# One state tile per direction in the RWKV-7 mixer, and its decays' running sums as TensorE products

## The chip, the cores and the metric

One core of a Trainium2 chip runs the whole kernel in one launch. The metric is device microseconds of that core, the median of three runs. TensorE is PE in the profile's rows, VectorE is DVE, ScalarE ACT, GpSimd POOL, SyncE SP; SP issues the loads.

## The reference, cut to what matters

A backbone of two layers over 256 context and 256 latent tokens, 1024 wide. Layer 0 is a Mamba-2 mixer with a dense SwiGLU, layer 1 a bidirectional RWKV-7 mixer ("mixer 2") with a top-2-of-8 expert SwiGLU. The change touches mixer 2 alone. For each direction d and each of 16 heads of 64 it computes

```python
logw = -0.606531 * sigmoid(w0[d] + tanh(xw @ w1[d]) @ w2[d])
a    = sigmoid(a0[d] + (xa @ a1[d]) @ a2[d])
kd   = k * (1 + (a - 1) * k_a)
...
sa = einsum('bhvk,bhk->bhv', S, kk_t)
S  = S * w_t - sa * (kk_t * a_t) + v_t * kd_t       # w_t = exp(logw_t)
y  = einsum('bhvk,bhk->bhv', S, r_t)
```

once over the context tokens, of which only the final states are kept, and once over the latent tokens, which start from these.

## The kernel before, in words

Mixer 2 works on 256 tokens in four chunks of 64 (c = 0 to 3 forwards, 3 to 0 backwards), on eight heads at a time (half hh, four tiles of 128 features, two heads of 64 in each: "par" 0 in rows 0 to 63 and par 1 in rows 64 to 127, `ROWS`). A unit j, hh is the context (j = 0) or the latent tokens (j = 1) with one half of the heads. Each unit has three parts. **A** (`stage`) makes the decays and the operands of all chunks and their gram matrices. **T** (`invert`) inverts the 64x64 triangular systems, a long chain of small VectorE steps and TensorE products. **S** (`scan`) takes the state through the four chunks. Several of these generators are woven by `weave`, and a scheduler then orders each engine's queue. The stages of the program are named by what is woven, with j and hh behind each letter: A00 (with the v features), A01T00, T01S00, F1S01 (with the features of the latent tokens), A10, T10, S10A11, T11, S11, then `finish` and the experts. S11 is woven with the output projection, which `finish` ends.

Part A, lines 1005 to 1113 of before. `lora(pi)` makes, for a pair of chunks (128 tokens), th = tanh of the w path and ta = tanh of the a path, with features on the partitions: for each of four feature tiles a product with hw (line 1013) and one with ha (line 1014), each followed by its own ScalarE tanh with the bias w0h (lines 1015, 1017). GpSimd makes th + 1 (line 1023). `decays(c)` then forms the running sum of th over the 64 tokens of one chunk with a VectorE scan (line 1043; smask restarts it at each tile), and ScalarE makes from it the decays Dp (line 1047), dc (line 1049) and the inverse (line 1050). `operands` multiplies these into KR and BK, `grams` (lines 1082, 1091) makes C and BT.

Part S, lines 1227 to 1288. The state of one direction is held in two tiles, Sz[d][0] with the heads of par 0 in rows 0 to 63 and zeros below, and Sz[d][1] the other way round; xz is held in the same way. Thus every product takes all 128 rows as its contraction and writes the 64 output rows of its head's half. For a step and direction: x = C^T Q + KR^T Sz into PSUM, copied to xz by VectorE (par 0, line 1245) and ScalarE (par 1, line 1246); u = Tt^T xz, copied to Q (lines 1263, 1264); the next state is a TensorE copy of Sz by an identity (two products of 256 columns) plus BT^T Q, scaled by dc into Sz (line 1274, twice). On latent tokens, also an output y.

The lora weights w_l2 come by SP (line 1305), in A00 into half of the tile "Tt"; the head selector hT (line 1365) goes into the other half and is read by `unit_keys` (line 841), which normalises the keys. `decay` and `rate` (lines 902, 919) write the factors hw and ha, 64 rows for each direction in 128-row tiles whose other rows are zero.

Of the kernel before, what the change touches and what calls it, by code (L numbers as in the profile page):

```python
# [19 lines left out]
D = 1024  # L20
# [45 lines left out]
def prepare(inp):  # L66
# [46 lines left out]
    a["w_l2"] = np.stack([g["rw_w2"][0].reshape(128, D), g["rw_a2"][0].reshape(128, D), g["rw_g2"][0]], axis=1)  # L113
# [24 lines left out]
def tile_backbone(ctx: ExitStack, tc: tile.TileContext, T, out: bass.AP, dbg=None, stop=99):  # L138
# [584 lines left out]
    for t in Sz[0] + Sz[1] + xz[0] + xz[1]:  # L723
        G.memset(t, 0.0)
# [121 lines left out]
    def features(up, F, names, MB, nraw, nsp, base, normed_all=None, vx=None, xs=None, later_x=None, raw=None, part=None, tail=None, eng=(V, G)):  # L846
# [55 lines left out]
        def decay(o):  # L902
            for d in range(2):
                S.activation(F["hw"][d][ROWS[d]], o[ROWS[d], :256], AF.Tanh)
# [12 lines left out]
            return late  # L917

        def rate(o):
            for d in range(2):  # L920
                S.copy(F["ha"][d][ROWS[d]], o[ROWS[d], :256])
# [74 lines left out]
    def stage(tp, rp, F, un, d, l2, nb, bks, tags, ready):  # L996
# [8 lines left out]
        def lora(pi):  # L1005
            ts = slice(128 * pi, 128 * pi + 128)
            th = tp.tile([128, 2, 4, 64], F32, name=f"th{d}")
            ta = tp.tile([128, 4, 128], F32, name=f"ta{d}", bufs=nb)
            kd = tp.tile([128, 4, 128], F32, name=f"kd{d}", bufs=nb)
            for i in range(4):  # L1010
# [11 lines left out]
                yield  # L1022
# [16 lines left out]
        def decays(c):  # L1039
            th = cur[c // 2][0]  # L1040
            cum = tp.tile([128, 4, 64], F32, name=f"cum{d}", bufs=2)
            e = 1 if d == 0 else -1
            V.tensor_tensor_scan(cum.rearrange("p k t -> p (k t)")[:, ::e], smask.rearrange("p k t -> p (k t)"),
                                 th[:, c % 2].rearrange("p k t -> p (k t)")[:, ::e], 0.0, op0=ALU.mult, op1=ALU.add)
            Dp = tp.tile([128, 4, 65], F32, name=f"Dp{d}", bufs=2)
            G.memset(Dp[:, :, 64 * d:64 * d + 1], 1.0)
            S.activation(Dp[:, :, o:o + 64], cum, AF.Exp, scale=-0.3032655)
            end = 63 * o
            S.activation(un.dc[d][:, :, c:c + 1], cum[:, :, end:end + 1], AF.Exp, scale=-0.3032655)
            S.activation(cum, cum, AF.Exp, scale=0.3032655)  # L1050
            return Dp, cum

        def operands(c, dd, slot):
            Dp, Di = dd
# [12 lines left out]
            return BK  # L1067
# [33 lines left out]
        dd = decays(od[0])  # L1101
        yield
        for i, c in enumerate(od):
            while not ready(i):
                yield
            BK = operands(c, dd, 2 * i + d)
            if i % 2 == 0 and j:
                bonus(od[i] // 2)
            if i == 1:
                yield from lora(od[2] // 2)  # L1110
            if i < 3:
                dd = decays(od[i + 1])
            yield
            yield from grams(c, BK, 2 * i + d)
# [112 lines left out]
    def scan(F, un, y=None):  # L1227
# [6 lines left out]
        for i in range(4):  # L1234
            st = []
            for d in range(2):
# [13 lines left out]
            for d in range(2):  # L1250
# [4 lines left out]
                if not (j and i == 3):  # L1255
                    for par in range(2):
                        mm(ba[ROWS[par], 0:256], ident[:, ROWS[par]], Z[par][:, ks, :].rearrange("p h v -> p (h v)"), first=True)
                if j:
                    for h, par in HP:
                        mm(py[ROWS[par], h, :], Z[par][:, k0 + h, :], KR[:, h, 64:128], first=i == 3 and h == 0)  # L1260
                for h, par in HP:
                    mm(pu[ROWS[par], h, :], un.Tt[:, d, 4 * c + h, :], xz[d][par][:, h, :], end=h == 3)
# [39 lines left out]
    def stages(tp, rp, F, un, nb, bks, tags, ready, l2=None):  # L1302
        if l2 is None:
            l2 = tp.tile([128, 2, 512], F32, name="l2")
        SY.dma_start(l2, T["w_l2"][:, :2, 512 * un.hh:512 * un.hh + 512])
# [12 lines left out]
    with ExitStack() as es:  # L1318
        f0 = es.enter_context(tc.tile_pool(name="f0", bufs=1, reuse_waits="tile"))
        F = {n: f0.tile([128, 8, 256], F32, name=n) for n in ("k", "kk")}  # L1320
        F.update({n: [f0.tile([128, 256], F32, name=f"{n}{d}") for d in range(2)] for n in ("hw", "ha")})
        for t in F["hw"] + F["ha"]:
            G.memset(t, 0.0)
# [23 lines left out]
        with tc.tile_pool(name="r00", bufs=1, side="right", reuse_waits="tile") as r00, tc.tile_pool(name="tp0", bufs=1, reuse_waits="tile") as tp:  # L1347
# [15 lines left out]
            l2 = held[:, 1].rearrange("p (a b) t -> p a (b t)", a=2)  # L1363
            hT = held[:16, 0].rearrange("p (k a) t -> p k (a t)", k=8)
# [7 lines left out]
            slots = {"T": ("BK00", [128, 1024]), "M0": ("l2", [128, 2, 512]), "M1": ("BK01", [128, 1024])}  # L1372
# [8 lines left out]
    if True:  # L1381
# [3 lines left out]
        F.update({n: [fk.tile([128, 256], F32, name=f"{n}{d}") for d in range(2)] for n in ("hw", "ha")})  # L1385
        for t in F["hw"] + F["ha"]:
            G.memset(t, 0.0)
# [12 lines left out]
        for d in range(2):  # L1400
            dump(f"S{d}", Sz[d][0])
# [130 lines left out]
    def start_half():  # L1532
# [3 lines left out]
        later(g2, T["w_l2"][:, 2, :], after)  # L1536
# [326 lines left out]
```

## Time and profile before

| | us |
|---|---|
| median of three runs | 2649.88 |
| lowest and highest | 2646.11, 2653.32 |
| the profiled execution's own time | 2658.37 |
| its span in the trace | 2656.5 |
| TensorE busy | 2440.9 (92%) |
| VectorE busy | 2039.1 (77%) |
| ScalarE busy | 1457.5 (55%) |
| GpSimd busy | 341.9 (13%) |

The stages of mixer 2 stand in the trace at about these times: A00 985 to 1048, A01T00 to 1128, T01S00 to 1180, F1S01 to 1300, A10 to 1345, T10 to 1410, S10A11 to 1470, T11 to 1540, S11 to 1592 us. Layer 0 stands before 930 us, the experts after 1640. The granted clock of TensorE has two levels, 1.2 and 2.4 GHz; the profile gives it as a share of the higher one, so a stage's mean of 0.62 is a stretch mostly at the lower level. Read a timeline by its starts: the duration given for a group of matmuls contains a modelled tail of 0.2 to 0.3 us, and the next group may start within it.

### The profile page before, as it was taken

What the parts mean: (1) busy time and instruction counts of PE and PEld (TensorE: products, weight loads), DVE (VectorE), ACT (ScalarE), POOL (GpSimd) and SP (SyncE); (2) the same over time, 40 slices, a digit from 0 to 9 for tenths busy, and PEclk for the clock granted to TensorE, in tenths of its full rate; (3) what the DMA queues carried; (4) which work ended last, traced back from release to release, by engine and by line L of the source; (5) the groups of instructions that cost most, each with busy time, mean ns of one, the idle gap of its engine ahead of it and who ended that gap; (6) DMA issues with size and microseconds to landing.
All of it is one profiled execution on the core that took longest, in us unless ns stands there. A gap on an engine that the chain in (4) does not pass through costs nothing. (4 is left out here: it accounts for less than half of the span.)

```text
span 2656.5 us, 44879 instructions
## 1 busy us (share of the span) xinstructions
PE 2440.9 (92%) x17770; PEld 1994.8 (75%) x17770; DVE 2039.1 (77%) x3070; ACT 1457.5 (55%) x2322; POOL 341.9 (13%) x434
## 2 busy tenths in 40 slices
PE   7999998999999978679868797999999999999997
PEld 4777776878888767568767686887888788878875
DVE  5787888667554377687676645999999899989997
ACT  4454545333223265435335225877787777778775
POOL 1011102000000254233432211000000000000001
PEclk9999999999999978577888687999999999999999
DMA  7323232336564221022020116899999899989994
GB/s 260 120 88 102 74 104 80 122 121 201 169 203 140 85 94 48 16 68 80 18 73 2 59 39 265 318 359 341 359 370 358 327 363 368 357 320 368 367 340 158
DMA packets 99211, 511.63 MB, mean 193 GB/s; under 512 B 11648, under 2 KB 19072, under 8 KB 55216
## 3 DMA queue, kind: packets, MB, share of 16 engines
q1 hardware_dynamic: 97520, 506.52, 52.8%
q8 instruction: 141, 2.31, 0.4%
q10 hardware_dynamic: 1472, 2.16, 0.3%
q14 instruction: 78, 0.64, 0.1%
HBM read 506.54 MB, written 2.10 MB: 191 GB/s over the span
## 5 line engine op out<-in xcount | busy, mean ns | idle before, releaser
L1720 DVE TENSOR_TENSOR wlo<-wraw,whi 128x1024 fp32r<-128x1024 f32 x662 | 798.4, 1224 | 69.6 <-ACT whi L1719 49.1
L1719 ACT CAST whi<-wraw 128x1024 fp32r<-128x1024 f32 x662 | 694.3, 1051 | 207.1 <-PE gu L214 111.9
L213 PE MATMUL gu<-wlo,xg 128*128 128x512 f32 x896 | 355.3, 397 | 1.5 <-DVE wlo L1720 0.7
L214 PE MATMUL gu<-whi,xg 128*128 128x512 f32 x896 | 349.8, 391 | 0.0
L212 PE MATMUL gu<-whi,xg 128*128 128x512 f32 x896 | 336.4, 392 | 1.1 <-ACT xg L1739 0.9
L206 ACT CAST whi<-wraw 128x1024 fp32r<-128x1024 f32 (+2 forms) x126 | 129.7, 1030 | 218.4 <-PE acc L213 206.2
L207 DVE TENSOR_TENSOR wlo<-wraw,whi 128x1024 fp32r<-128x1024 f32 (+2 forms) x126 | 151.8, 1205 | 110.0 <-ACT whi L206 109.8
L213 PEld LDWEIGHTS gu<-wlo,xg 128*128 128x128 f32 x896 | 168.5, 188 | 42.3 <-DVE wlo L1720 6.1
L212 PEld LDWEIGHTS gu<-whi,xg 128*128 128x128 f32 x896 | 168.4, 188 | 38.1 <-ACT xg L1739 1.6
L214 PEld LDWEIGHTS gu<-whi,xg 128*128 128x128 f32 x896 | 168.7, 188 | 31.5
L213 PE MATMUL y<-wlo,HT 128*128 128x512 f32 x448 | 178.4, 398 | 2.3 <-DVE wlo L1720 2.0
L212 PE MATMUL y<-whi,HT 128*128 128x512 f32 x448 | 176.6, 396 | 3.0 <-DVE xg L1740 3.0
L214 PE MATMUL y<-whi,HT 128*128 128x512 f32 x448 | 176.1, 393 | 0.0
L212 PE MATMUL acc<-h2hi,whi 128*128 128x512 f32 x352 | 137.4, 393 | 3.4 <-ACT h2hi L343 3.4
L1794 POOL TENSOR_TENSOR wraw<-yx,SH 128x512 f32<-128x512 f32 x4 | 7.5, 1875 | 1022.1 <-DVE yx L1790 1022.1
L213 PE MATMUL acc<-h2lo,whi 128*128 128x512 f32 x352 | 137.4, 391 | 0.0
L212 PE MATMUL acc<-hhi,whi 128*128 128x512 f32 (+1 forms) x328 | 135.8, 414 | 0.8 <-ACT whi L206 0.8
L214 PE MATMUL acc<-h2hi,wlo 128*128 128x512 f32 x352 | 134.7, 391 | 0.3 <-DVE wlo L207 0.3
L213 PE MATMUL acc<-hlo,whi 128*128 128x512 f32 (+1 forms) x328 | 134.1, 409 | 0.0
L214 PE MATMUL acc<-hhi,wlo 128*128 128x512 f32 (+1 forms) x328 | 133.6, 408 | 0.0
L305 POOL TENSOR_TENSOR sqa<-sqa,sq 128x512 f32<-128x512 f32 (+1 forms) x35 | 47.5, 1357 | 579.2 <-issue 311.3
L260 DVE SCALAR_TENSOR_TENSOR wraw<-wraw,scb 128x1024 f32<-128x1024 f32 x56 | 68.5, 1223 | 50.2 <-DMA wraw<-in_w_modT_dram 49.4
(565 smaller groups left out, 5358.5 us busy)
## 6 DMA issues: line engine op xcount, KB each, us to landing
wraw<-in_w_mi_dram SPq DMA_DIRECT2D x219, 1024.0 KB, 5.0
wraw<-in_w_mo_dram SPq DMA_DIRECT2D x112, 1024.0 KB, 5.0
wraw<-in_w_modT_dram SPq DMA_DIRECT2D x56, 512.0 KB, 3.9
wraw<-in_w_ffi_dram SPq DMA_DIRECT2D x44, 512.0 KB, 3.6
wraw<-in_w_mod_dram SPq DMA_DIRECT2D x40, 512.0 KB, 5.0
wraw<-in_w_mb_dram SPq DMA_DIRECT2D x40, 512.0 KB, 4.8
wraw<-in_w_mbo_dram SPq DMA_DIRECT2D x16, 512.0 KB, 4.1
wraw<-in_w_ffo_dram SPq DMA_DIRECT2D x16, 512.0 KB, 3.6
```

Of the source, the lines that this page charges most:

```text
L206: S.copy(hi, raw)
L207: eng[q % len(eng)].tensor_sub(lo, raw, hi.bitcast(F32))
L212: PE.matmul(o, whi, xhi, start=start, stop=False)
L213: PE.matmul(o, whi, xlo, start=False, stop=False)
L214: PE.matmul(o, wlo, xhi, start=False, stop=stop)
L260: V.scalar_tensor_tensor(t, w, 0.5, scb[:, j, :], op0=ALU.mult, op1=ALU.mult, accum_out=mods[l][:, n, j:j + 1])
L305: G.tensor_add(self.acc, self.acc, sq)
L1719: S.copy(hi, raw[:, k:k + 2, :])
L1720: V.tensor_sub(lo, raw[:, k:k + 2, :], hi.bitcast(F32))
L1794: G.tensor_mul(xf[:, tt, 512 * n:512 * n + 512], fs, fg[:, 512 * n:512 * n + 512])
```

## The change

In part A: w0 and a0 become a 65th row of w_l2, against a row of ones in hw and ha, so that the tanh needs no bias. hw of both directions and ha lie in rows 0 to 63. One product of 128x512 (line 1012 of after) gives the w path with tokens on the partitions, four of 128x128 give the a path in one bank, and each has one tanh of 128x512. The running sums are four products for a pair of chunks and a direction, of th with a constant triangular matrix (tb_f, tb_b, line 1049); the three exponents read their PSUM bank, 512 wide, once for two chunks. The scan's mask and the w0h constants go. In part S: one Sz and one xz tile for each direction, the two halves below each other; products with them contract over the 64 rows of their head; xz is copied by heads (VectorE two, ScalarE two, 128 rows each); one copy product and one update of 128x256 for a step and direction. The head selector goes into the tile "M1".

```diff
+    a["w_l2"] = np.stack([np.stack([np.concatenate([g["rw_" + n + "2"][0][d], g["rw_" + n + "0"][0][d][None]])
+                                    for n in ("w", "a")], axis=1) for d in range(2)], axis=1)
...
+    same = (j < 64) == first
+    for n, v in (("tb_f", same & (r <= cc)), ("tb_b", same & (r >= cc)), ("m_f0", mf * sign[0]), ("m_f1", mf * sign[1]), ("m_b0", mb * sign[0]), ("m_b1", mb * sign[1]),
...
-    Sz = [[rc.tile([128, 8, 64], F32, name=f"Sz{d}{par}") for par in range(2)] for d in range(2)]
-    xz = [[rc.tile([128, 4, 64], F32, name=f"xz{d}{par}") for par in range(2)] for d in range(2)]
+    Sz = [rc.tile([128, 8, 64], F32, name=f"Sz{d}") for d in range(2)]
+    xz = [rc.tile([128, 4, 64], F32, name=f"xz{d}") for d in range(2)]
...
+            p = ms()
+            PE.matmul(p, F["hw"][d][:, ts], l2[:65, d, 0], start=True, stop=True)
+            S.activation(flat(th), p, AF.Tanh, scale=0.5)
+            p = ms()
+            for i in range(4):
+                PE.matmul(p[:, 128 * i:128 * i + 128], l2[:65, d, 1, 128 * i:128 * i + 128], F["ha"][d][:, ts],
+                          start=True, stop=True)
+            S.activation(flat(ta), p, AF.Tanh, scale=0.5)
+            yield
             for i in range(4):
                 k = k0 + i
-                p = ms()
-                PE.matmul(p[:, 0:128], l2[:, 0, 128 * i:128 * i + 128], F["hw"][d][:, ts], start=True, stop=True)
-                PE.matmul(p[:, 128:256], l2[:, 1, 128 * i:128 * i + 128], F["ha"][d][:, ts], start=True, stop=True)
-                S.activation(th[:, :, i, :], p[:, 0:128].rearrange("p (c t) -> p c t", c=2), AF.Tanh,
-                             bias=w0h[:, 8 * d + k:8 * d + k + 1], scale=0.5)
-                S.activation(ta[:, i, :], p[:, 128:256], AF.Tanh, bias=w0h[:, 16 + 8 * d + k:17 + 8 * d + k], scale=0.5)
...
-            V.tensor_tensor_scan(cum.rearrange("p k t -> p (k t)")[:, ::e], smask.rearrange("p k t -> p (k t)"),
-                                 th[:, c % 2].rearrange("p k t -> p (k t)")[:, ::e], 0.0, op0=ALU.mult, op1=ALU.add)
...
+        def decays(pi):
+
+            th = cur[pi][0]
+            p = ms()
+            for i in range(4):
+                PE.matmul(p[:, 128 * i:128 * i + 128], th[:, i, :], K2["tb_" + "fb"[d]], start=True, stop=True)
+            cum = p.rearrange("p (k c t) -> p k c t", k=4, c=2)
...
+            S.activation(Dp[:, :, :, o:o + 64], cum, AF.Exp, scale=-0.3032655)
+            S.activation(un.dc[d][:, :, 2 * pi:2 * pi + 2], cum[:, :, :, 63 * o], AF.Exp, scale=-0.3032655)
...
+            S.activation(Di, cum, AF.Exp, scale=0.3032655)
...
-                    mm(px[ROWS[par], h, :], KR[:, h, 0:64], Z[par][:, k0 + h, :], end=h == 3)
-                V.tensor_copy(xz[d][0][ROWS[0]], px[ROWS[0]])
-                S.copy(xz[d][1][ROWS[1]], px[ROWS[1]])
+                    mm(px[ROWS[par], h, :], KR[ROWS[par], h, 0:64], Z[ROWS[par], k0 + h, :], end=h == 3)
+                V.tensor_copy(xz[d][:, 0:2], px[:, 0:2])
+                S.copy(xz[d][:, 2:4], px[:, 2:4])
...
-                    for par in range(2):
-                        mm(ba[ROWS[par], 0:256], ident[:, ROWS[par]], Z[par][:, ks, :].rearrange("p h v -> p (h v)"), first=True)
+                    mm(ba[:, 0:256], ident, Z[:, ks, :].rearrange("p h v -> p (h v)"), first=True)
...
-                    mm(pu[ROWS[par], h, :], un.Tt[:, d, 4 * c + h, :], xz[d][par][:, h, :], end=h == 3)
+                    mm(pu[ROWS[par], h, :], un.Tt[ROWS[par], d, 4 * c + h, :], xz[d][ROWS[par], h, :], end=h == 3)
...
-                    for par in range(2):
-                        V.tensor_tensor(Z[par][ROWS[par], ks], pz[ROWS[par]],
-                                        un.dc[d][ROWS[par], :, c:c + 1].to_broadcast([64, 4, 64]), op=ALU.mult)
+                    V.tensor_tensor(Z[:, ks], pz, un.dc[d][:, :, c:c + 1].to_broadcast([128, 4, 64]), op=ALU.mult)
...
-            hT = held[:16, 0].rearrange("p (k a) t -> p k (a t)", k=8)
+            hT = tp.tile([128, 1024], F32, name="M1")[:16].rearrange("p (k f) -> p k f", k=8)
```

The scheduler orders each queue anew. The first place is TensorE near the end of S11, where the state products (xu from Sz and KR, line 1233 before and 1238 after) of the last step meet the output products (acc from C and Q). Before, all of them contract over 128 rows:

```order
L1233 MATMUL xu<-Sz_7482,KR_14504 64x64
L1233 MATMUL acc<-C_12284,Q_12270 64x64
L1233 MATMUL xu<-Sz_7481,KR_14504 64x64
L1233 MATMUL acc<-C_12285,Q_12271 64x64
L1233 MATMUL xu<-Sz_7482,KR_14504 64x64
L1233 MATMUL acc<-C_12284,Q_12270 64x64
L1233 MATMUL xu<-Sz_7481,KR_14504 64x64
L1233 MATMUL acc<-C_12285,Q_12271 64x64
```

After, at the same place, the products with Sz contract over 64 rows and those with C still over 128:

```order
L1238 MATMUL xu<-Sz_7476,KR_14222 64x64
L1238 MATMUL acc<-C_12126,Q_12112 64x64
L1238 MATMUL xu<-Sz_7476,KR_14222 64x64
L1238 MATMUL acc<-C_12127,Q_12113 64x64
L1238 MATMUL xu<-Sz_7476,KR_14222 64x64
L1238 MATMUL acc<-C_12126,Q_12112 64x64
L1238 MATMUL xu<-Sz_7476,KR_14222 64x64
L1238 MATMUL acc<-C_12127,Q_12113 64x64
```

The two kinds take turns in both orders; what moved is the shape, which now changes at every row. Counted over the whole program, the shape of consecutive products (contraction and output rows, in steps of 32, 64 and 128) changes 459 times before and 616 times after.

The second place is TensorE in A01T00, where the inversion's products (line 1192 before, 1197 after: ms from M and T) share the queue with the lora products of the second pair of chunks (1013, 1014; after 1012, 1016) and, after, with the running sums (1049: xu from the constants c and th). Before:

```order
L1192 MATMUL ms<-M_9414,T 32x16 x18
L1013 MATMUL xu<-hw_7502,l_9098 128x128
L1014 MATMUL xu<-ha_7504,l_9098 128x128
L1192 MATMUL ms<-M_9414,T 32x16 x2
L1013 MATMUL xu<-hw_7503,l_9098 128x128
L1014 MATMUL xu<-ha_7505,l_9098 128x128
L1192 MATMUL ms<-M_9414,T 32x16 x13
```

After:

```order
L1197 MATMUL ms<-M_9312,T 32x16 x5
L1012 MATMUL xu<-l_9028,hw_7488 128x512
L1197 MATMUL ms<-M_9312,T 32x16 x10
L1016 MATMUL xu<-ha_7490,l_9028 128x128 x4
L1197 MATMUL ms<-M_9312,T 32x16 x9
L1049 MATMUL xu<-c_7463,th_9248 128x128 x4
L1197 MATMUL ms<-M_9312,T 32x16 x9
L1049 MATMUL xu<-c_7463,th_9264 128x128 x4
L1197 MATMUL ms<-M_9312,T 32x16 x31
```

The eight lora steps of before (two of them shown) became two, one for each direction, and the eight running-sum products entered between the inversion's products.

The third place is SP's queue ahead of A00. Before, the head selector (Tt from the constants) is loaded early:

```order
L769 DMA wraw<-in_w_k_dram 128x1024 x5
L1365 DMA Tt<-in_cs_dram 16x1024
L1305 DMA Tt<-in_w_l_dram 128x2x512
L769 DMA wraw<-in_w_k_dram 128x1024
L769 DMA wraw<-in_w_lora_dram 128x4x128 x4
L769 DMA T<-in_w_v_dram 128x1024
```

After:

```order
L768 DMA wraw<-in_w_k_dram 128x1024 x5
L1307 DMA Tt<-in_w_l_dram 65x4x512
L768 DMA wraw<-in_w_k_dram 128x1024
L768 DMA wraw<-in_w_lora_dram 128x4x128 x4
L1367 DMA M_8221<-in_cs_dram 16x1024
L768 DMA T<-in_w_v_dram 128x1024
```

The head selector, now into M1, stands directly ahead of the first w_v load.

## Rows read from the trace of the kernel before

**Rows 1.** Windows by stage: us; PE, PEld, DVE, ACT, POOL busy; PEclk, DMA, GB/s.

```profile
985.00:1048.00 63.00, 56.54 (x791) 49.60 (x790) 41.56 (x83) 38.20 (x107) 37.72 (x59) 0.86 0.20 69
1048.00:1128.00 80.00, 47.60 (x1172) 41.73 (x1164) 58.05 (x158) 38.28 (x109) 17.73 (x37) 0.62 0.04 13
1128.00:1180.00 52.00, 32.13 (x567) 27.99 (x568) 44.86 (x109) 15.82 (x37) 15.20 (x20) 0.76 0.15 47
1180.00:1280.00 100.00, 96.59 (x1113) 86.25 (x1113) 71.24 (x137) 50.00 (x115) 36.64 (x40) 0.78 0.27 85
1280.00:1345.00 65.00, 49.68 (x970) 41.47 (x966) 46.48 (x84) 23.72 (x81) 34.48 (x50) 0.84 0.01 2
...
1410.00:1470.00 60.00, 52.75 (x1002) 44.53 (x997) 42.29 (x81) 29.10 (x89) 21.62 (x33) 0.91 0.01 2
1470.00:1540.00 70.00, 55.12 (x972) 43.83 (x972) 44.12 (x128) 20.09 (x45) 8.57 (x11) 0.62 0.16 56
1540.00:1592.00 52.00, 50.95 (x876) 44.86 (x872) 23.85 (x61) 16.14 (x40) 12.60 (x16) 0.92 0.13 43
```

**Rows 2.** Waits of PE in S11: us in total, times, longest.

```profile
PE xu L1233 <- ACT xz L1246: 0.8, 1, 0.8
PE xu L1233 <- DVE Q L1264: 0.2, 1, 0.2
```

**Rows 3.** Groups by line: count, ns min/median/max, first and last start, forms.

```profile
L1043 DVE TENSOR_TENSOR_SCAN cum<-smask,th x32: 657/682/1684, 998.3 to 1452.9; 128x256 f32<-128x256 f32 x32
...
L1274 DVE TENSOR_TENSOR Sz<-acc,dc x56: 390/422/429, 1135.8 to 1580.2; 64x256 f32<-64x256 f32 x56
...
L1245 DVE COPY xz<-xu x32: 381/417/418, 1129.2 to 1582.1; 64x256 f32<-64x256 f32 x32
...
L1015 ACT ACTIVATE th<-ms,w0h x32: 346/368/417, 989.8 to 1447.0; 128x128 f32<-128x128 f32 x32
...
L1476 ACT ACTIVATE sqh<-ms x4: 597/597/597, 1504.7 to 1594.1; 128x512 f32<-128x512 f32 x4
```

**Rows 4.** Timeline of PE in S11: start, us (with modelled tail), operation, count.

```profile
1549.81 0.34 PE L1233 MATMUL acc<-Q,BT 128*64 128x64 f32 x4
1549.93 0.34 PE L1233 MATMUL xu<-Q,C 128*64 128x64 f32 x4
...
1551.03 0.28 PE L1233 MATMUL acc<-C,Q 128*64 128x64 f32 x2
1551.24 0.33 PE L1491 MATMUL ms<-cst,rx 128*128 128x128 f32 x1
```

**Rows 5.** The same view in A00: grams on all four quarters of the array.

```profile
1032.10 0.63 PE L1082 MATMUL acc<-KR,BK 64*64 64x64 f32 x30
```

**Rows 6.** The same view at the start of the last scan, within T11.

```profile
1523.18 0.31 PE L1216 MATMUL acc<-M,T 32*32 32x32 f32 x2
1523.42 0.47 PE L1233 MATMUL acc<-KR,Sz 128*64 128x64 f32 x2
1523.82 0.31 PE L1216 MATMUL acc<-M,T 32*32 32x32 f32 x2
...
1534.68 1.07 PE L1233 MATMUL xu<-Sz,KR 128*64 128x64 f32 x16
1535.68 1.91 PE L1216 MATMUL xu<-M,T 32*32 32x32 f32 x62
```

**Rows 7.** The same view in A10: the lora products.

```profile
1302.10 0.39 PE L1013 MATMUL xu<-hw,l 128*128 128x128 f32 x2
1302.33 0.39 PE L1014 MATMUL xu<-ha,l 128*128 128x128 f32 x2
```

**Rows 8.** Timeline of DVE in A01T00, within the inversion.

```profile
1062.64 1.26 DVE L1043 TENSOR_TENSOR_SCAN cum<-smask,th 128x256 f32<-128x256 f32 x2
1063.82 0.49 DVE L1164 TENSOR_TENSOR M<-T,M 128x252 f32<-128x252 f32 x2
```

**Rows 9.** Waits of DVE in A01T00: us in total, times, longest.

```profile
DVE M L1194 <- PE ms L1192: 9.9, 1, 9.9
```

More of the change, by code (lines that the diff above doesn't have):

```diff
@@ L112, in prepare @@
     a["w_g1"] = _tiles(w[:, 256:], [[(0, 128)]])[0]
-    a["w_l2"] = np.stack([g["rw_w2"][0].reshape(128, D), g["rw_a2"][0].reshape(128, D), g["rw_g2"][0]], axis=1)
+    a["w_l2"] = np.stack([np.stack([np.concatenate([g["rw_" + n + "2"][0][d], g["rw_" + n + "0"][0][d][None]])
+                                    for n in ("w", "a")], axis=1) for d in range(2)], axis=1)
+    a["w_g2"] = g["rw_g2"][0]
     a["w_ro"] = _tiles(g["rw_out_w"][0], [[(256 * n_, 256 * n_ + 256)] for n_ in range(4)])
@@ L718, in tile_backbone @@
     ROWS = (slice(0, 64), slice(64, 128))
-    Sz = [[rc.tile([128, 8, 64], F32, name=f"Sz{d}{par}") for par in range(2)] for d in range(2)]
-    xz = [[rc.tile([128, 4, 64], F32, name=f"xz{d}{par}") for par in range(2)] for d in range(2)]
-    for t in Sz[0] + Sz[1] + xz[0] + xz[1]:
+    Sz = [rc.tile([128, 8, 64], F32, name=f"Sz{d}") for d in range(2)]
+    xz = [rc.tile([128, 4, 64], F32, name=f"xz{d}") for d in range(2)]
+    for t in Sz:
         G.memset(t, 0.0)
@@ L920, in rate @@
             for d in range(2):
-                S.copy(F["ha"][d][ROWS[d]], o[ROWS[d], :256])
+                S.copy(F["ha"][d][:64], o[ROWS[d], :256])
         def value(n):
@@ L1037, in bonus @@
             V.tensor_add(F["bon"][:, ts], F["bon"][:, ts], p[:16, :128])
[L1039 to L1042, printed above, removed]
-            V.tensor_tensor_scan(cum.rearrange("p k t -> p (k t)")[:, ::e], smask.rearrange("p k t -> p (k t)"),
-                                 th[:, c % 2].rearrange("p k t -> p (k t)")[:, ::e], 0.0, op0=ALU.mult, op1=ALU.add)
[L1045 to L1051, printed above, removed]
+        def decays(pi):
[4 more added lines that the diff above has]
+            cum = p.rearrange("p (k c t) -> p k c t", k=4, c=2)
+            Dp = tp.tile([128, 4, 2, 65], F32, name=f"Dp{d}")
+            G.memset(Dp[:, :, :, 64 * d:64 * d + 1], 1.0)
+            S.activation(Dp[:, :, :, o:o + 64], cum, AF.Exp, scale=-0.3032655)
+            S.activation(un.dc[d][:, :, 2 * pi:2 * pi + 2], cum[:, :, :, 63 * o], AF.Exp, scale=-0.3032655)
+            Di = tp.tile([128, 4, 2, 64], F32, name=f"cum{d}")
+            S.activation(Di, cum, AF.Exp, scale=0.3032655)
+            return Dp, Di
         def operands(c, dd, slot):
-            Dp, Di = dd
+            Dp, Di = (t[:, :, c % 2] for t in dd)
             _, ta, kd = cur[c // 2]
@@ L1100, in stage @@
         yield from lora(od[0] // 2)
-        dd = decays(od[0])
+        dd = decays(od[0] // 2)
         yield
@@ L1110, in stage @@
                 yield from lora(od[2] // 2)
-            if i < 3:
-                dd = decays(od[i + 1])
+                dd = decays(od[2] // 2)
             yield
@@ L1255, in scan @@
                 if not (j and i == 3):
-                    for par in range(2):
-                        mm(ba[ROWS[par], 0:256], ident[:, ROWS[par]], Z[par][:, ks, :].rearrange("p h v -> p (h v)"), first=True)
+                    mm(ba[:, 0:256], ident, Z[:, ks, :].rearrange("p h v -> p (h v)"), first=True)
                 if j:
                     for h, par in HP:
-                        mm(py[ROWS[par], h, :], Z[par][:, k0 + h, :], KR[:, h, 64:128], first=i == 3 and h == 0)
+                        mm(py[ROWS[par], h, :], Z[ROWS[par], k0 + h, :], KR[ROWS[par], h, 64:128], first=i == 3 and h == 0)
                 for h, par in HP:
-                    mm(pu[ROWS[par], h, :], un.Tt[:, d, 4 * c + h, :], xz[d][par][:, h, :], end=h == 3)
+                    mm(pu[ROWS[par], h, :], un.Tt[ROWS[par], d, 4 * c + h, :], xz[d][ROWS[par], h, :], end=h == 3)
                 S.copy(Q[0][ROWS[0], c, ks], pu[ROWS[0]])
@@ L1303, in stages @@
         if l2 is None:
-            l2 = tp.tile([128, 2, 512], F32, name="l2")
-        SY.dma_start(l2, T["w_l2"][:, :2, 512 * un.hh:512 * un.hh + 512])
+            l2 = tp.tile([128, 2, 2, 512], F32, name="l2")
+        SY.dma_start(l2[:65], T["w_l2"][:, :, :, 512 * un.hh:512 * un.hh + 512])
         return [(stage(tp, rp, F, un, d, l2, nb, bks, tags[d], ready), 1) for d in range(2)]
@@ L1320, in tile_backbone @@
         F = {n: f0.tile([128, 8, 256], F32, name=n) for n in ("k", "kk")}
-        F.update({n: [f0.tile([128, 256], F32, name=f"{n}{d}") for d in range(2)] for n in ("hw", "ha")})
+        F.update({n: [f0.tile([65, 256], F32, name=f"{n}{d}") for d in range(2)] for n in ("hw", "ha")})
         for t in F["hw"] + F["ha"]:
-            G.memset(t, 0.0)
+            G.memset(t[64:], 1.0)
         rs = f0.tile([16, 256], F32, name="rs")
@@ L1362, in tile_backbone @@
             held = r01.tile([128, 2, 16, 64], F32, name="Tt")
-            l2 = held[:, 1].rearrange("p (a b) t -> p a (b t)", a=2)
-            hT = held[:16, 0].rearrange("p (k a) t -> p k (a t)", k=8)
+            l2 = held.rearrange("p d (a b) t -> p d a (b t)", a=2)
+            hT = tp.tile([128, 1024], F32, name="M1")[:16].rearrange("p (k f) -> p k f", k=8)
             SY.dma_start(hT, T["cs2"][:16, CS2["hselT"]:].rearrange("p (k f) -> p k f", k=8))
@@ L1384, in tile_backbone @@
         F.update({n: fk.tile([128, 8, 256], F32, name=n) for n in ("k", "kk", "r")})
-        F.update({n: [fk.tile([128, 256], F32, name=f"{n}{d}") for d in range(2)] for n in ("hw", "ha")})
+        F.update({n: [fk.tile([65, 256], F32, name=f"{n}{d}") for d in range(2)] for n in ("hw", "ha")})
         for t in F["hw"] + F["ha"]:
-            G.memset(t, 0.0)
+            G.memset(t[64:], 1.0)
         uxs = ctx.enter_context(ExitStack())
@@ L1535, in start_half @@
         later(hT, T["cs2"][:16, CS2["hselT"]:].rearrange("p (k f) -> p k f", k=8), after)
-        later(g2, T["w_l2"][:, 2, :], after)
+        later(g2, T["w_g2"], after)
         later(wr, T["w_rt"], after)
```

19 lines of the change are left out of this document (8 added, 11 removed).

## The prediction

> **What bounds the kernel now.** I read the table by stage first, because only mixer 2 (about 985 to 1640 us) is touched and its stages have different limits. [rows 1] gives one line for each stage that matters: busy time of TensorE, VectorE, ScalarE and GpSimd, then the granted clock. Two stages are TensorE from end to end: F1S01 (96.6 of 100 us) and S11 (51.0 of 52). The waits of TensorE in S11 confirm it: 1.0 us in all [rows 2]. A00 is nearly so (56.5 of 63), S10A11 too (52.8 of 60). A01T00, T01S00 and A10 are chains in which no engine is full and the clock is 0.62 to 0.84.
>
> Then I read the groups that go [rows 3]: the scans of line 1043 (32, median 0.682 us on VectorE), the state updates of line 1274 (56 of 64x256, 0.422), the copies of line 1245 (32 of 64x256, 0.417), the tanh of line 1015 (32 here, 32 more in the other bank and 64 like them in line 1017, 0.368). Removed from VectorE: 32 x 0.68 = 21.8 us of scans and 28 x 0.42 = 11.8 us of updates. ScalarE does 32 wide tanh instead of 128; line 1476 is the nearest row for one (128x512 out of PSUM, 0.597), so 128 x 0.368 = 47.1 us become 32 x 0.6 = 19.1. Neither engine bounds a stage, so these sums are worth what stands on a chain.
>
> Last I read how TensorE steps from product to product, since the change alters the shape of many. Each fp32 product is two instructions.
>
> **The change part by part, against the profiled execution.**
>
> *Half-height products.* The products of state and xz now use 64 rows (the half their data lies in) where they used 128 with zeros. Is a 64-row product cheaper? In S11 at full clock, 128-row products with 64 columns start four in 0.12 us, 0.03 us each [rows 4]: even and odd heads go to different columns and overlap in pairs. The grams of line 1082 do 30 instructions in 0.63 us [rows 5], 0.02 each with the tail, but those use all four quarters of the array; the scan's loop alternates two, the diagonal ones, and keeps the pairs it had. I take no gain. The Trainium skill, TensorEngine Tiling (Array Packing), section Theoretical Speedup, puts a small dimension of at most 64 at up to twice the speed; by it the sum below would be near -5, by these rows it is +4.5 (rival 3 is the mechanism).
>
> What changes is the succession. Before, state, xz and Q products all have one shape and mix freely; now 64-row ones alternate with 128-row ones, one by one in many places. Rows that show alternation: at the start of S11's work (half clock) two instructions of a 32x32 product and two of a 128x64 one take turns, 1523.18 to 1523.82, 0.64 us a turn; the same without turns: 62 in 1.91 us and 16 in 1.07 us [rows 6], so 2 x 0.031 + 2 x 0.067 = 0.20. A turn has two changes of shape: 0.22 each at half clock. At full clock: two instructions of a 128x64 product at 1551.03, the 128x128 one at 1551.24 [rows 4]: 0.21 for what takes 0.06 unmixed, so 0.15 for a lone product; a change after a full pair spares the lost overlap, nearer 0.09. I take 0.12, ends 0.09 and 0.22.
>
> In the new order I count the changes of shape among the scan's stretches: T01S00 from 3 to 35, F1S01 20 to 45, S10A11 72 to 76, S11 56 to 156.
>
> - S11: 100 x 0.12 = +12 on an engine that waits 1.0 us; that 1 us may go. **+11** (9 to 15; below that if the alternating products fall into waits, +6).
> - F1S01: 25 x 0.12 = +3, less a part of the 3.4 us TensorE is free there. **+2.5** (0 to 5.5).
> - T01S00: 32 x 0.12 = +3.8, up to 7 at half clock; a latency chain, TensorE on it. Gained per step and direction: one update of 0.42 instead of two in a row [rows 3], and a copy of 128 elements for one of 256 on both engines. The 128-wide copies have no row here; between nothing and half of 0.417 saved, I take 0.14 on VectorE and 0.1 on ScalarE. Four steps x (0.42 + 0.24) = 2.6 for one direction, 5.2 if both lie in series. **0** (-3 to +4).
>
> *One copy product and one update per direction.* 56 copies of 64 rows become 28 of 128. The two 64-column copies of before overlap, so TensorE gains nothing: none. The updates are counted above.
>
> *Decays.* Sixteen (pair, direction) groups add four 128x128 fp32 products: two instructions take 0.22 us at full clock (1302.10 to 1302.33) [rows 7], twice that at half. 64 x 0.22 to 0.44 = 14 to 28 us over four stages, 3.5 to 7 each. The w products keep their columns (64 of 128 become 16 of 512): nothing. The exponents read PSUM 512 wide, once for two chunks; the bank is held through three of them.
>
> - A00: TensorE is busy 56.5 of 63 us; 3.5 to 7 of new products fill what is left, while the scans leave its tail. **0** (-2 to +4). On SP's queue the head selector's load moves behind the w_k and lora loads and ahead of the first w_v load (rival 4); w_l2 moves one place up, early enough either way.
> - A01T00: eight scans of 0.68 = 5.4 us go from VectorE. Two of four early ones stand inside the inversion's chain at 1062.64 [rows 8], directly between two of its steps. The longest wait there is 9.9 us, VectorE on TensorE's line 1192 [rows 9], which sits behind the lora products in the queue; their tanh shrink (16 x 0.368 to 4 x 0.6, -3.5) but eight new products at half clock (3.5) now wait for GpSimd ahead of part of line 1192. That cancels. **-4** (-8 to 0).
> - A10: eight scans of 0.68 on the chain of VectorE, -5.4; against it the new products, 0.9 to 1.7 each group, between GpSimd's th and the first exponent, which is wider. **-3** (-6 to +2).
> - S10A11: scans -5.4 on VectorE and three updates of 0.42 fewer for each direction, on the state's chain; new products +3.5 on TensorE, at 52.8 of 60 us, which hides little. **-2** (-6 to +3).
>
> The memsets and the removed constants lie on GpSimd, which is at most 60% busy (A00, 37.7 of 63 us): none. The 513 KB instead of 385 KB of constants load early in layer 0: none.
>
> **Sum:** 0 - 4 + 0 + 2.5 - 3 - 2 + 11 = **+4.5 us**: 2662.9 against this execution's 2658.4. It is 8.5 above the median of the runs, 2649.9; against that, **2654.4 us**.
>
> **The rivals.**
>
> 1. *The clock falls in S11* (the slower side of mine, decided by the alternating products). T11, where TensorE is busy 55.1 of 70 us with small products, has 0.62, S11 0.92 [rows 1]. If the turns keep S11 at T01S00's 0.76, its 51 us take 51 x 0.92 / 0.76 = 62, and changes cost up to 0.22: +10 or more on top, **2664**. For it: at 1523 to 1528 the turns ran at half clock throughout. Against: the output projection stands between the turns.
>
> 2. *The decays pay in full and the turns hide.* A01T00 -8, A10 -6, S10A11 -4, S11 only +6, F1S01 +2.5: **2640**. For it: every engine but TensorE loses work, and three of the stages are chains. Against: TensorE's queue is in order, and S11 has 1.0 us of waits to hide in [rows 2].
>
> 3. *Half-height products run twice as fast.* A scan has 8 state and 8 xz products for each direction and step, 8 more for the output in the pass over the latent tokens: 256 instructions in F1S01, 384 in S11. At half of 0.03 us saved that is 640 x 0.015 = 9.6 less: **2645**. Against: in the rows only products on all four quarters come below 0.03 [rows 5]. The rule of the Trainium skill named above, TensorEngine Tiling (Array Packing), Theoretical Speedup, would make this the forecast.
>
> 4. *The head selector is late in A00.* Its load now waits for the memory of the v mixing, so the normalised-key products wait, and the w_v load behind it on SP's queue moves too. Nothing in the rows prices it; below by nothing, above by about the 6.5 us that TensorE is free in A00: +6, **2660**.
>
> **How the numbers follow.** Forecast 0.47 (its own range 2646 to 2662), rival 1 0.22, rival 2 0.17, rival 3 0.07, rival 4 0.07. A measurement can tell 0.3%, 8 us, from no change: below 2642 is faster, above 2658 slower. Faster: most of rival 2, a little of rival 3 and of the forecast's lower end, 0.17. Slower: rival 1, most of rival 4 and the upper end of the forecast, 0.36. Same: 0.47. The range takes the rivals in to their times and a little past rival 1, whose price is open upward: 2640 to 2668.
>
> **What would show it.** Right: S11 of the changed kernel is 60 to 66 us long at a clock near 0.9, with TensorE still without waits, and lone 64-row and 128-row products about 0.2 us apart where they take turns; F1S01 2 to 3 us longer; A01T00 and A10 shorter by a few us each, with no scan on VectorE. Wrong: S11 no longer than before although its products alternate (the price of a turn is then wrong), or 64-row products four to 0.06 us (rival 3), or T01S00 shorter by more than 4 us. If A01T00 is not shorter, the new products have taken the scans' place in front of line 1192.

## The result and the profile after

The changed kernel took **2672.8 us** (median of 5, 2665.0 to 2677.4), the kernel before beside it 2646.1: ratio **1.0091, interval 1.0067 to 1.0114**. The forecast was 2654.4 in a range of 2640 to 2668; the measured time lies above the range. The profiled execution after took 2672.77 us (span 2670.7).

The table by stage, in the columns of [rows 1], the same stages in the same order (A00 and A01T00 are divided at 1048 in both tables: the last gram of A00, line 1091 before and 1097 after, starts at 1048.0 and 1048.3):

```profile
985.00:1048.00 63.00, 59.40 (x773) 50.68 (x776) 40.54 (x73) 30.96 (x68) 34.08 (x52) 0.86 0.25 78
1048.00:1122.00 74.00, 51.56 (x1192) 43.71 (x1188) 53.02 (x156) 31.31 (x74) 16.62 (x35) 0.64 0.05 15
1122.00:1172.00 50.00, 35.51 (x555) 29.93 (x555) 38.32 (x94) 14.59 (x37) 14.62 (x20) 0.77 0.15 48
1172.00:1272.00 100.00, 97.20 (x1095) 85.16 (x1095) 70.10 (x136) 50.95 (x115) 37.02 (x38) 0.78 0.28 85
1272.00:1338.00 66.00, 58.41 (x980) 44.79 (x978) 38.93 (x72) 18.48 (x48) 32.79 (x48) 0.87 0.02 4
...
1400.00:1460.00 60.00, 57.88 (x1034) 46.61 (x1029) 31.44 (x66) 23.44 (x63) 18.55 (x28) 0.89 0.01 2
1460.00:1531.00 71.00, 55.73 (x1013) 44.31 (x1010) 44.41 (x131) 20.92 (x47) 10.91 (x15) 0.65 0.21 70
1531.00:1608.00 77.00, 76.25 (x845) 61.13 (x847) 19.82 (x54) 14.42 (x40) 12.62 (x16) 0.81 0.09 29
```

One line stands out: S11, 77 us instead of 52, TensorE busy in 76 of them, at 0.81 instead of 0.92. No other row is longer by more than a microsecond; cut at the copies of xz, as below, S10A11 is longer by 2.7. The waits of TensorE in S11 are as short as before [rows 2], so nothing new is waited for; TensorE itself needs longer:

```profile
PE xu L1238 <- ACT xz L1251: 0.6, 1, 0.6
PE xu L1238 <- DVE Q L1268: 0.2, 1, 0.2
```

The other engines' work shrank as the prediction took it to. The groups that answer to [rows 3] (the scan group is gone):

```profile
L1277 DVE TENSOR_TENSOR Sz<-acc,dc x28: 408/425/427, 1128.7 to 1586.2; 128x256 f32<-128x256 f32 x28
...
L1250 DVE COPY xz<-xu x32: 248/292/293, 1121.9 to 1595.5; 128x128 f32<-128x128 f32 x32
...
L1013 ACT ACTIVATE th<-ms x8: 590/597/598, 988.6 to 1437.0; 128x512 f32<-128x512 f32 x8
```

Why TensorE needs longer stands in its timeline in S11 of the changed kernel (columns as in [rows 4]): first at half clock, then at full clock.

```profile
1538.80 0.47 PE L1238 MATMUL xu<-Sz,KR 64*64 64x64 f32 x2
1539.20 0.47 PE L1238 MATMUL acc<-C,Q 128*64 128x64 f32 x2
1539.61 0.47 PE L1238 MATMUL xu<-Sz,KR 64*64 64x64 f32 x2
...
1554.36 0.32 PE L1238 MATMUL xu<-Sz,KR 64*64 64x64 f32 x2
1554.61 0.33 PE L1238 MATMUL acc<-C,Q 128*64 128x64 f32 x2
1554.87 0.33 PE L1238 MATMUL xu<-Sz,KR 64*64 64x64 f32 x2
```

Where the two shapes take turns, a product starts every 0.26 us at full clock and every 0.40 at half (1.2 GHz). Unmixed, eight such products (x16) follow in 0.61 at full clock (a row of an experiment, below), 0.08 each. So a lone product, one with the other shape before and behind it, pays 0.18 more at full clock. The Trainium skill, TensorEngine Tiling (Array Packing), section Key Properties, says that "Changing tiling mode (not just tile) drains the TensorE"; the trace agrees, with this price for it.

The two traces of before and after differ by 14 us and the medians by 27, so a second trace of the kernel before was taken (below).

### The profile page after: what moved, and what is told of

It reads as the page before. It is cut to its first block, busy times and chain, and to the rows that moved or that the text cites. A ratio compares the mean times of both kernels' runs of the same rounds, so it can differ in the third digit from the quotient of the medians.

```text
span 2670.7 us, 44560 instructions
## 1 busy us (share of the span) xinstructions
PE 2487.1 (93%) x17746; PEld 2014.1 (75%) x17746; DVE 2003.2 (75%) x3009; ACT 1427.3 (53%) x2178; POOL 330.5 (12%) x410
## 5 line engine op out<-in xcount | busy, mean ns | idle before, releaser
L219 PE MATMUL acc<-h2hi,wlo 128*128 128x512 f32 x352 | 134.6, 391 | 0.3 <-DVE wlo L212 0.3
L780 POOL TENSOR_TENSOR wlo<-wraw,whi 128x512 fp32r<-128x512 f32 (+1 forms) x69 | 87.1, 1271 | 179.6 <-ACT whi L779 159.4
```

What stands on the lines that cost most here:

```text
L219: PE.matmul(o, wlo, xhi, start=False, stop=stop)
L780: self.eng[self.n % len(self.eng)].tensor_sub(lo, raw, hi.bitcast(F32))
```

## The experiments

For the comparisons mixer 2 is cut where the timeline of VectorE shows the copies of xz: the 1st, 9th, 16th, 17th, 24th, 25th and last of 32. "T11" and "S11" here are the 24th to 25th and the 25th to last. In us:

| | before | before, 2nd | after | scan_only | decays_only | full_rows | grouped_200 | decays_grouped_2 |
|---|---|---|---|---|---|---|---|---|
| up to the first | 1129.2 | 1128.9 | 1121.9 | 1127.8 | 1118.3 | 1120.1 | 1117.6 | 1120.3 |
| S00 | 33.1 | 34.3 | 33.0 | 34.0 | 34.0 | 29.3 | 32.6 | 34.3 |
| F1S01 | 135.6 | 134.0 | 136.6 | 134.6 | 126.6 | 132.2 | 135.6 | 127.0 |
| A10, T10 | 103.3 | 103.5 | 101.5 | 103.0 | 100.9 | 101.4 | 101.6 | 101.1 |
| S10A11 | 59.9 | 59.7 | 62.6 | 57.5 | 60.8 | 57.5 | 62.6 | 55.8 |
| T11 | 74.8 | 73.8 | 70.8 | 67.6 | 71.6 | 70.1 | 66.5 | 63.5 |
| S11 | 46.3 | 40.9 | 69.1 | 70.9 | 41.2 | 44.2 | 44.0 | 41.6 |
| rest | 1074.4 | 1074.0 | 1075.2 | 1072.5 | 1074.5 | 1069.2 | 1077.8 | 1074.8 |

The expectations of scan_only, sz_one, full_rows and the first decays_only give S11 by the longer cut of the stage table (52 us before and 77 in the change, where this table has 46 and 69).

The theory after the result: changes of shape on TensorE, and the clock that they keep down, cost it all. The rivals: the decays cost, or the wide updates and copies, or half-height products as such.

**1. The one-tile scan alone, on the kernel before (scan_only).**

```diff
-    Sz = [[rc.tile(... name=f"Sz{d}{par}") for par in range(2)] for d in range(2)]
+    Sz = [rc.tile(... name=f"Sz{d}") for d in range(2)]
...
-  mm(px[ROWS[par], h, :], KR[:, h, 0:64], Z[par][:, k0 + h, :], end=h == 3)
+  mm(px[ROWS[par], h, :], KR[ROWS[par], h, 0:64], Z[ROWS[par], k0 + h, :], end=h == 3)
...
```

> The kernel before with the scan's part of the change alone: one state tile and one xz tile per direction, the products that read them over 64 rows; decays as before. Theory (each change between products of 128 rows and of 64 rows costs TensorE 0.20 us at the full clock, 0.30 us at half): against the kernel before, 104 more such changes in S11 and 32 more in T01S00, so S11 takes 73 to 82 us instead of 52, S00 some 5 us more, in all 2670 to 2686 us. Rival 1 (what costs is the decays on TensorE, which put it late into each scan): 2642 to 2650 us, S11 52 us. Rival 2 (the clock that fell in S11 is due to a TensorE left idle by the changed stages ahead of it, not to the scan): S11 at the granted clock of before, under 60 us.

2669.0 us, ratio 1.0062 (1.0038 to 1.0085). The scan carries the loss: S11 takes 70.9 us without the decays too, so they are not what lengthens it. The total is 1 us under the theory's band, and S00 grew by 1 us at most, not 5: that part of the theory failed. S11 of this kernel, by window:

```profile
1525.00:1595.00 70.00, 69.25 (x765) 55.72 (x762) 17.74 (x47) 12.69 (x34) 12.63 (x16) 0.79 0.10 31
```

**2. Only the state in one tile (sz_one), only xz in one tile (xz_one).** The other half of the scan's part is left as before.

> The kernel before with one state tile per direction but xz still in two: 155 more changes of shape than before in the whole program, 88 of them in S11, 29 in T01S00. Theory (changes of shape): 0.20 to 0.30 us for each of the 88 in S11, so S11 70 to 78 us, S00 4 to 6 us more, total 2664 to 2680 us, just under the kernel with both in one tile. Rival 1 (the products of Tt with xz, which stand last in each step, carry the cost): within 6 us of the kernel before, 2645 to 2652 us. Rival 2 (each of the two carries half): 2655 to 2662 us.

> The kernel before with xz in one tile and the state still in two: 37 more changes of shape than before in the whole program, 10 in S11, 8 in T01S00. Theory (the cost goes by the number of changes): 1 to 3 us in S11, under 1.5 us in S00, the total within 5 us of the kernel before, 2645 to 2658 us. Rival (64-row products cost by themselves, 64 of them in S11): 6 us or more in S11, 2660 us or above.

sz_one: 2676.0 us, 1.0095 (1.0071 to 1.0118), with S11 66 us at 0.84. The state's products carry the cost in S11. Two parts of the theory failed: S00 took 34.3 us, no more than in the second trace of before, and the total is 7 us above the kernel with both in one tile (scan_only), not just under it. In its trace S11 is shorter than there, but S10A11 takes 67 us at 0.81 of the clock where scan_only has 57.5 at 0.97, at no more work (54 us at full clock against 56). xz_one: 2661.3 us, 1.0044 (1.0026 to 1.0062), a miss for the theory, and a total in the rival's band, though not by the rival's way: S11 is 4 us longer than in the second trace of before, not 6 or more, for ten more changes, where up to 3 were expected. Some of it came over the cut from T11, whose work fell from 48 to 46 us at full clock; most of the rest is S10A11, 67 us at 0.81, where the kernel before had 60 at 0.93. Its rows:

```profile
1402.00:1469.00 67.00, 60.95 (x1019) 52.09 (x1021) 37.36 (x72) 31.57 (x97) 17.37 (x28) 0.81 0.01 2
...
1542.00:1587.00 45.00, 44.34 (x827) 39.59 (x822) 23.66 (x67) 14.36 (x38) 12.55 (x16) 1.00 0.15 49
```

**3. The changed kernel without the changes of shape (full_rows).**

```diff
-  mm(px[ROWS[par], h, :], KR[ROWS[par], h, 0:64], Z[ROWS[par], k0 + h, :], end=h == 3)
+  mm(px[ROWS[par], h, :], KR[:, h, 0:64], Z[:, k0 + h, :], end=h == 3)
...
```

> The changed kernel, but the products that read the state tile or xz take all 128 rows of it, and the copy of the state into the accumulator is two products of 64 columns: the same tiles, the same wide copies and updates, the same decays, and no more changes of shape than in the kernel before (447 in all, before has 459, the change 616). It mixes the two heads of a tile, so its output is not the reference's. Theory (changes of shape): S11 comes back to 48 to 56 us, the total to 2632 to 2645 us. Rival 1 (the one-tile form itself costs: one 128-row update in place of two halves, copies that both directions' heads wait for): S11 stays above 70 us, 2664 to 2676 us. Rival 2 (half and half): 2650 to 2660 us.

2627.5 us, 0.9915 (0.9893 to 0.9936), 5 us under the theory's band. With products of one height the one-tile form costs nothing: S00 is shorter by 4 us (29.3) and S11 is back at 44.2. That excludes the wide form as the cause. Whether it is a gain in all is not shown: the decays without it (decays_only, below) took 2631.1 on the same chip, and the two intervals overlap.

```profile
1511.00:1555.00 44.00, 43.24 (x782) 38.38 (x775) 18.80 (x48) 12.82 (x34) 12.60 (x16) 0.92 0.16 50
```

**4. The changed kernel with its half-height products in whole groups (grouped_200; grouped with a weaker raise).**

```diff
-                for h, par in HP:
-                    mm(px[ROWS[par], h, :], KR[ROWS[par], h, 0:64], Z[ROWS[par], k0 + h, :], end=h == 3)
+                with tc.high_priority(200):
+                    for h, par in HP:
+                        mm(px[ROWS[par], h, :], KR[ROWS[par], h, 0:64], Z[ROWS[par], k0 + h, :], end=h == 3)
...
```

> The changed kernel, with a higher scheduling priority for the groups of eight products over 64 rows (state by KR, Tt by xz), so that each group stands together on TensorE: 529 changes of shape instead of 616, in S11 79 instead of 156, in T01S00 31 instead of 35. Nothing else differs: one tile, wide copies and updates, the same products. Theory (0.15 us a change at the full clock, and the clock that falls with it): 77 fewer in S11 give 11.5 us at the full clock and some 5 us of clock, so S11's scan, 69 us in the change, takes 50 to 56 us, the total 2650 to 2660 us. Rival (half-height products cost by themselves, wherever they stand): S11 stays above 64 us, the total 2666 to 2680 us.

> The changed kernel with a default raise of the priority of the same three groups: the grouping is only partial, 569 changes of shape instead of 616, 130 in S11 instead of 156 (the stronger raise had 79). Theory (cost by the number of changes, 0.15 to 0.20 us each at full clock): S11's work at full clock, 55 us in the change and 40 us with 79 changes, is 49 to 52 us, and the total lies between the two, 2655 to 2668 us. Rival (the order only matters once the groups stand whole): S11 as in the change, 54 to 56 us at full clock, the total 2665 to 2675 us.

grouped_200: **2640.4 us, 0.9968 (0.9953 to 0.9983)**: the same products, the same tiles, 30 us less than the change, by their order alone. S11 takes 44.0 us, less than the theory's 50 to 56, and the total is 10 us under its band. Its timeline shows the groups unmixed, eight products of 64 rows in 0.61 us, the change behind them included, and eight of 128 rows (1539.18 to 1539.70) in 0.52, with more of their own shape behind them:

```profile
1537.94 0.70 PE L1238 MATMUL acc<-Sz,cst 128*128 128x256 f32 x2
1538.57 0.68 PE L1238 MATMUL acc<-KR,Sz 64*64 64x64 f32 x16
1539.18 0.69 PE L1238 MATMUL acc<-Q,BT 128*64 128x64 f32 x16
1539.70 0.40 PE L1238 MATMUL acc<-C,Q 128*64 128x64 f32 x6
```

Where a change follows both, as in the trace of grouped, eight products of either height take 0.61:

```profile
1584.39 0.68 PE L1238 MATMUL xu<-Sz,KR 64*64 64x64 f32 x16
1585.00 0.69 PE L1238 MATMUL acc<-C,Q 128*64 128x64 f32 x16
1585.61 0.68 PE L1238 MATMUL xu<-Sz,KR 64*64 64x64 f32 x16
```

Half-height products are thus no faster and no slower; their neighbours decide. grouped: 2662.0 us, 1.0031 (1.0012 to 1.005), between the two as the theory had it, but S11 has 53 us at full clock instead of 49 to 52. Of its twelve runs four lie at 2649.0 to 2651.5 and eight at 2659.4 to 2666.1, where the trace is from, so the median stands for neither group well. Its timeline shows what remains dear: lone products, 0.26 (1547.50 to 1547.76), and two of one shape that follow one another, 0.37 (1547.13 to 1547.50):

```profile
1545.46 0.33 PE L1238 MATMUL acc<-KR,Sz 64*64 64x64 f32 x4
1545.72 0.33 PE L1238 MATMUL acc<-Q,BT 128*64 128x64 f32 x2
1545.98 0.33 PE L1238 MATMUL acc<-KR,Sz 64*64 64x64 f32 x2
1546.24 0.33 PE L1238 MATMUL xu<-Q,C 128*64 128x64 f32 x2
...
1547.13 0.32 PE L1238 MATMUL xu<-xz,Tt 64*64 64x64 f32 x2
1547.29 0.28 PE L1238 MATMUL acc<-KR,Sz 64*64 64x64 f32 x2
1547.50 0.33 PE L1238 MATMUL acc<-Q,BT 128*64 128x64 f32 x2
1547.76 0.32 PE L1238 MATMUL xu<-xz,Tt 64*64 64x64 f32 x2
```

**5. The decays alone (decays_only), and with the raised priority (decays_grouped).** The scan is that of before, with its products over 128 rows in the same three groups.

```diff
-            Di = tp.tile([128, 4, 2, 64], F32, name=f"cum{d}")
+            Di = th.rearrange("p k (c t) -> p k c t", c=2)
...
-            l2 = tp.tile([128, 2, 2, 512], F32, name="l2")
+            l2 = [tp.tile([128, 2, 512], F32, name=f"l2{x}") for x in "ab"]
...
```

> The change's other part alone: running sums as TensorE products, constants in a 65th row, and the scan with two state tiles as before. To fit the memory the inverse decays overwrite the tile of the tanh, and the second lora weights come in two transfers. Theory: the decays' gain up to the start of S11 (9 to 10 us in the two traces) stays and S11 is as before, 50 to 54 us: 2632 to 2642 us, faster than both. Rival 1 (the decays' gain is given back in the scans, which start earlier but are bound by what else runs beside them): 2643 to 2650 us. Rival 2 (the decays themselves cost and the one-tile scan is innocent): over 2660 us.

> The decays' part alone (scan with two state tiles, all its products over 128 rows) with the same higher priority for the same three groups of products as in the kernel with the grouped order. The number of changes of shape hardly moves (445 against 454; S11 55 against 56). Theory (grouping helped by saving changes): no gain from it here, S11's scan 39 to 47 us at 40 to 41 us of full clock, the total 2625 to 2640 us, as without the priority. Rival (the priority itself shortens the scan, by its chain of waits): S11's work at full clock falls as far as it fell with the grouped one-tile scan, by 10 us or more, and the total to 2620 us or less.

> The decays alone once more, beside the same kernel with the raised priority. Expected 2627 to 2638 us; T11, from the last xz copy of the scan before to the first of S11, 70 to 73 us, some 47 us of it at full clock, with 53 changes of shape.

> The decays alone with the raised priority once more. Theory (in T11 the early products of the last scan no longer alternate with the inversion's 32x32 ones: 23 fewer changes of shape there, at 0.2 us each 4 to 5 us at full clock, 6 to 9 us at the clock of that stage): T11 62 to 66 us, S11 40 to 43 us, the total 5 to 10 us under that of the kernel without the priority. Rival (the 8 us in T11 were that trace's clock): the totals within 3 us of each other.

decays_only: 2631.1 us, 0.9932 (0.9909 to 0.9955), and 2633.6, 0.995 (0.9936 to 0.9964): under the band of the theory by a microsecond at first, inside at the second time. decays_grouped: 2624.9, 0.991 (0.9883 to 0.9938), and **2624.7, 0.9927 (0.9906 to 0.9947)**, 9 us less than decays_only on the same chip and the fastest version that computes the reference. S11 is as long with the raised priority as without (41.6 against 41.2): the priority by itself does nothing there, as the theory had it. T11 gives 7 to 8 us (71.6 and 70.2 against 63.2 and 63.5, in the theory's 62 to 66): in decays_only early products of the last scan alternate with the inversion's 32x32 ones, as in [rows 6]; in decays_grouped they stand apart, and T11 has 30 changes of shape instead of 53. S10A11 is shorter too, 55.8 us at 0.98 of the clock in both traces against 60.8 and 61.0 at 0.84, with more work at full clock (55 us against 51), so that part is clock, which the theory did not have. First decays_only, then decays_grouped, both at half clock:

```profile
1500.07 0.47 PE L1238 MATMUL acc<-KR,Sz 128*64 128x64 f32 x2
1500.47 0.31 PE L1221 MATMUL acc<-M,T 32*32 32x32 f32 x2
1500.71 0.47 PE L1238 MATMUL acc<-KR,Sz 128*64 128x64 f32 x2
```

```profile
1489.85 1.07 PE L1238 MATMUL acc<-KR,Sz 128*64 128x64 f32 x16
1490.84 1.86 PE L1221 MATMUL acc<-M,T 32*32 32x32 f32 x61
```

**6. Both kernels once more (after_again, before_again).** No edit.

> The changed kernel once more, beside the others on one chip: 2665 to 2677 us, as at its first measurement; S11 at a granted clock of 0.78 to 0.83 if the clock in S11 belongs to this kernel, near 0.9 if it was chance.

> The kernel before once more, for a second trace: its runs lie between 2643 and 2658 us, and the trace at hand is of one at the upper end. If the difference of 10 us is one stage's granted clock, one stage alone is shorter in a trace of a run near 2645 us, with the same busy time at full clock.

The change: 2670.2 us, 1.0076 (1.006 to 1.0092), S11 again 69 us at 0.80. The kernel before: 2650.8 us with a span of 2649.0. S11 by window, in the second trace of before, in the first one, and in the change (here cut where its clock changes):

```profile
1534.00:1575.00 41.00, 40.02 (x796) 36.25 (x790) 21.26 (x56) 13.97 (x34) 12.59 (x16) 1.00 0.17 54
```

```profile
1536.00:1548.00 12.00, 12.00 (x172) 10.81 (x169) 5.31 (x15) 2.61 (x7) 0.00 (x0) 0.50 0.01 3
1548.00:1582.00 34.00, 33.02 (x620) 29.89 (x619) 15.80 (x40) 11.37 (x27) 12.60 (x16) 1.00 0.19 64
```

```profile
1526.00:1550.00 24.00, 24.00 (x230) 18.84 (x228) 6.09 (x18) 3.51 (x11) 0.61 (x2) 0.50 0.01 1
1550.00:1590.00 40.00, 39.24 (x516) 32.44 (x516) 10.87 (x28) 8.79 (x21) 12.00 (x14) 1.00 0.17 54
1590.00:1602.00 12.00, 12.00 (x129) 9.97 (x127) 2.10 (x6) 1.18 (x4) 0.00 (x0) 0.57 0.00 1
```

The trace on which the prediction was built had 12 us of half clock in S11, the second none: 5.4 us of the 7.5 between them. The change has 24, and the clock falls again at its end.

Length times granted clock gives S11's work at full clock: before 41 x 1.00 = 41 (46 x 0.87 = 40 in the first trace), after 69 x 0.80 = 55, scan_only 70 x 0.79 = 55, sz_one 66 x 0.84 = 55, grouped 55 x 0.97 = 53, grouped_200 44 x 0.90 = 40, decays_only 41 x 1.00, xz_one 45 x 1.00. Changes of shape, counted in TensorE's records of that stretch: 23 before, 121 after, 123, 109, 94, 53, 23 and 33. So 98 more changes make 14 us, **about 0.15 each at full clock**; the other 14 us of the difference to 41 are clock.

## Why the prediction was wrong

The step that failed is the term for S11, **+11 (9 to 15)**, which priced the changes of shape and took the clock of one trace as given. Between the traces S11 is +22.8, against the second trace of before +28.2: 14 us of work, for which the term had 12, and 14 of clock, for which it had nothing.

- *Its mechanism was right.* Undone alone (full_rows, grouped_200) or made alone (scan_only, sz_one), the changes of shape take 25 us from S11 or bring it 20 to 30.
- *Its price was a little low.* 0.12 us a change against 0.15 measured: the row at 1551.03 in [rows 4] ends a long stretch of its own shape and has a change only behind it, where a lone product has one on either side and pays 0.18. That gives 14 instead of 12, still inside the bounds.
- *The clock was left to a rival, and the rival was added up too low.* Rival 1 put S11 at 0.76; it came to 0.80, with 24 us at half clock at its start instead of 0 or 12. I priced S11 at the 0.92 of one trace. Rival 1's own terms are 62 - 51 = 11 for the old work and 100 x (0.22 - 0.12) = 10 for the changes, 21 on top of the forecast and 2675; it entered 10 of them, 2664, and the range ended at 2668.
- *The sum of all else held, in part by luck.* Forecast -6.5; measured 14.2 - 22.8 = -8.6, and 21.7 - 28.2 = -6.5 against the second trace. Up to the first xz copy -7 (A00 and A01T00: -4; by the stage table all of it is A01T00's), F1S01 +1 (+2.5), A10 and T10 -2 (-3), S00 0 (0). The zero of S00 is two terms that cancel as forecast: without the changes of shape (full_rows) it has 29.3, so the wide form gains 4 (2.6 to 5.2) and the changes cost 4 (3.8). S10A11 was +2.7 instead of -2: its work fell (60 x 0.93 = 56 to 63 x 0.84 = 53 at full clock), its clock more. T11, which had no term, lost 4 and made up for that by luck.
- *The base.* The sum was set against the median of 2649.9, and the trace's own run was 8.5 above it, mostly by the half clock in S11. Against a trace at full clock S11 begins 5 us shorter, and the same S11 after it is a term 5 us larger.
- *Rival 2's first half* was true by itself: the decays gain 13 to 18 us alone. Rival 3 is false: eight products take 0.61 us at either height, so the rule on small dimensions in the Trainium skill, TensorEngine Tiling (Array Packing), section Theoretical Speedup, gives nothing for these two diagonal tiles. Rival 4: the products of the normalised keys did start later, the last at 1010.1 instead of 1005.2, but A00's last grams stand where they stood, so it cost nothing.

The parts do not add up: 16 us for the scan alone and -13 to -18 for the decays alone, by the ratios, make about nothing, and the change is +20 to +24. By the table, 9 us of this are F1S01, which has 127 us in the two-tile kernels with new decays and 136.6 in the change, at the same work at full clock (127 x 0.88 = 112, 137 x 0.80 = 110); 5 are T11, 5 lie before the first xz copy and 4 are S10A11. Why is not shown.

*Open:* why the clock comes back so late in S11 of the change. It stayed at half for the first 23 to 24 us in three traces of one-tile scans (after, after_again, scan_only), but for 13 in sz_one, with 109 changes, and for none in grouped, with 94 (3.5 us later on); kernels with 23 changes had 0 to 12. No run held the changes fixed and moved the clock. So what the changes cost in work is shown; that they keep the clock down is argued. Nor does the count alone set the price: 27 changes fewer (grouped) saved 2 us at full clock, the next 41 (grouped_200) 14, and grouped_200, with 53, has no more work than the kernel before with 23. One reason is in the traces: two products of one shape between changes take 0.26 us if they start together and 0.37 if one follows the other. In S11 at full clock 8 of 9 such pairs start together in the change, 3 of 19 in grouped.

## What to carry to other kernels

Where products of different tile shapes share TensorE's queue, count the lone ones and pay about 0.2 us for each at full clock; a smaller product that fills its half exactly can cost more than one padded with zeros. Put products of one shape in unbroken groups before judging a layout: here that order alone was worth 30 us, and with two state tiles another 9, both with their part of clock; groups left half open were worth 10. Read the granted clock of the stage in more than one trace before pricing a TensorE-bound stage, and set the sum against a trace whose clock is known.

## What the hardware showed that was not expected

- A product of 64 rows takes a slot of 0.26 us between products of another shape, and so do two of them that start together: in the rows of grouped above, four instructions at 1545.46 are followed by the next shape at 1545.72, as two instructions are at 1545.98 by 1546.24. Two that follow one another take 0.37 (1547.13 to 1547.50). Products of 128 rows do the same (0.26 and 0.38).
- The same stage of the same kernel runs at 1.00 or at 0.87 of the clock from trace to trace (S11 of before, 41 and 46 us; decays_only, on two chips, 41 and 46 us at 1.00 and 0.88).
- A stage can be shorter by 9 us with no less work at full clock: F1S01 with the new decays and two state tiles:

```profile
1152.00:1279.00 127.00, 110.40 (x1490) 97.89 (x1488) 100.89 (x187) 65.44 (x150) 56.69 (x64) 0.88 0.25 80
```
